# Moving the modulation chunks, the context entrance and two norms in a float32 model kernel

## The chip, the cores and the metric

One core of one Trainium2 chip runs the whole program. The metric is device microseconds of one execution; 2544.06 us is the median of three runs of the kernel before. The engines that matter here are PE (TensorE: matmuls, weight loads listed apart as PEld), ACT (ScalarE), DVE (VectorE) and SP, whose queue issues the loads.

## The reference, cut to what matters

256 tokens of 1024 channels pass through two parts. `first_block` is one layer: a norm, projections, a recurrence (`rwkv`) and a state-space branch (`s5`), gates, `w_out`, and a convolutional feed-forward:

```python
x = x + rms_norm(mixed, norm_mix_post[l])
h = rms_norm(x, norm_ffn_pre[l])
f = conv_ffn(h, ffn_w_up[l], ffn_conv_w[l], ffn_conv_b[l], ffn_w_down[l])
x = x + rms_norm(f, norm_ffn_post[l])
```

`second_block` has two layers with a second stream of 256 context tokens. Their inputs are modulated, `x * (1 + scale) + shift`, by `mod = silu_c @ w_ada[l] + b_ada[l]` (6144 values a layer, for the latent and for the context). Each layer has a linear attention (GLA), a latent attention (MLA), a 31-tap convolution, gates, an output projection and a feed-forward. All arithmetic is float32 in effect.

## The kernel before, in words

Activations are kept transposed: channels on the 128 partitions, tokens along the row (256, or 512 with the context as columns 256 to 511). Every dense product is three matmuls (`mm3`, L312 to L314), because both operands are split into a float32r high part and the rest: `w_high x_high + w_high x_low + w_low x_high`. A weight block of 512 KB is loaded into one of four `wraw` buffers, cast by ACT (`wh`, L276) and subtracted by DVE (`wl`, L277) into one of three pairs of buffers.

The modulation weights are 24 chunks of 512 columns (`ada`, L1035). A chunk is four `wraw` loads of 512 KB and eight matmuls of a 128x32 stationary tile with 512 columns (L1051), dealt to four column groups; the trace has 16 records for them. Up to LOTS = 4 chunks share one end: a copy of the row (L1057), four matmuls that fold it (8 records, L1061), small adds into `mod`. `ada` is a generator that yields after each half chunk. The chunks run in this order: 17 in lots of four beside the recurrence (`fill`, L442, called 62 times by `rwkv`; of three calls two advance `ada` and two the gate columns), one ahead of block 1's feed-forward (L508, `ADA[1]`), one between block 1 and layer 0 (L1806, `ADA[2]`), and one in each of the first five heads of layer 0's MLA (`beside`, L1218).

Block 1's end goes: `post` (L535) projects with `w_out`, scales and squares each tile on ACT, sums the squares over channels on PE (`colsum`, L363), then `rms_of` (L370) makes the reciprocal root in 11 small DVE operations and spreads it over 128 partitions by two transposes (L368). Eight times, two DVE operations then update X (L550, L551), and with `more` ACT squares X (L522) and PE sums again. `block1_ffn` makes its own root from these sums, `rms_in` (L525) normalises and splits X into `hh`, `hl` (L531, L304, L305), and `f_up` begins.

`enter` (L1782) modulates a stream and splits it into `hx`, the input of layer 0 (L1786, L304, L305). `enter(context, 1)` stands ahead of `block1_ffn` and loads the context through three buffers; `enter(X, 0)` stands behind it. Layer 0 begins with `conv_in` (L1354), whose first product is followed by `start` of `gla_gates` (L1446: `w_misc`); both are 512 columns wide.

The order on an engine isn't that of the text. The build puts it together from dependences and free buffers, earlier text first, so that an operation of later text stands ahead when the earlier one is not ready. `issue_after` adds an order edge.

Of the kernel before, what the change touches and what calls it, by code (L numbers as in the profile page):

```python
# [15 lines left out]
I32 = mybir.dt.int32  # L16
AF = mybir.ActivationFunctionType
# [4 lines left out]
P = 128  # L22
D = 1024
KT = 8
# [11 lines left out]
ADA = (17, 1, 1)  # L36
# [91 lines left out]
def const_arrays():  # L128
# [16 lines left out]
    c.raw("bcol", b2)  # L145

# [45 lines left out]
class Body:  # L192
# [23 lines left out]
    @contextmanager  # L216
    def behind(self, work):

        bb = self.nc.cur_bb
        n = len(bb.bb.instructions)  # L220
        work()
        mine = [i for i in bb.bb.instructions[n:] if i.engine == mybir.EngineType.DVE]
        if not mine:
            yield
            return
        with self.tc.issue_after(mine[-1]):
            yield

# [152 lines left out]
    def block1(self, X, xp):  # L381
# [4 lines left out]
        with ExitStack() as es:  # L386
# [52 lines left out]
            ada = self.ada(ADA[0], "sy", LOTS)  # L439
# [38 lines left out]
            return self.post(bp, X, "w_out", self.pairs(mh, ml), 0.5, "norm_mix_post", True)  # L478

    def block1_ffn(self, X, pc):  # L480
# [3 lines left out]
        with ExitStack() as es:  # L484
            bp = es.enter_context(tc.tile_pool(name="b1f", bufs=1))
            tp = es.enter_context(tc.tile_pool(name="b1ft", bufs=3))
            hh, hl = self.rms_in(bp, X, "norm_ffn_pre", self.rms_of(pc, 2, D, EPS))
# [20 lines left out]
            self.ada_all(ADA[1])  # L508
            self.dense("f_up", range(FT), self.pairs(hh, hl), epi_up)
            self.post(bp, X, "f_dn", self.pairs(gh, gl), 1.0, "norm_ffn_post", False)  # L510
# [9 lines left out]

    def squares(self, pc, X, sq, k):
        self.nc.scalar.activation(sq[:, k], X[:, k], AF.Square)  # L522
        self.colsum(pc, sq[:, k], k == 0, k == KT - 1)
# [11 lines left out]
    def post(self, bp, X, wname, x, scale, gname, more):  # L535

        nc = self.nc
        y, sq = self.b8(bp), self.b8(bp)
        pc = self.psum(2, "aux")

        def epi(m, ps):
            nc.scalar.activation(y[:, m], ps, AF.Copy, scale=scale)
            nc.scalar.activation(sq[:, m], ps, AF.Square, scale=scale)
# [4 lines left out]
        pc = self.psum(2, "aux") if more else None  # L548
        for k in range(KT):
            nc.vector.scalar_tensor_tensor(y[:, k], y[:, k], self.vc(1, gname, k), R, ALU.mult, ALU.mult)  # L550
            nc.vector.tensor_tensor(X[:, k], X[:, k], y[:, k], ALU.add)  # L551
            if more:
                self.squares(pc, X, sq, k)
        return pc
# [516 lines left out]
    def ada_all(self, n):  # L1071
        for _ in self.ada(n):
            pass

# [78 lines left out]
    def layer(self, l, g, mod, xd, xo, nxt, late):  # L1153
# [53 lines left out]
        with ExitStack() as es:  # L1207
            ya = self.gla(l, pool(es, "gla"), hx, hq, hb, V, full, *g.decay)
# [145 lines left out]
    def conv_in(self, l, pool, g, V, full, beside):  # L1354
# [79 lines left out]
    def gla_gates(self, l, pool, lp, hx, hb, V):  # L1434
# [11 lines left out]
        def start():  # L1446
            nc.sync.dma_start(wa, self.ap[f"w_wa{l}"])
            self.dense(f"w_misc{l}", [0], hx, lambda m, ps: nc.scalar.activation(misc, ps, AF.Identity, bias=V("b_misc", 0)))
# [42 lines left out]
    def gla(self, l, gp, hx, hq, hb, V, full, FB, Bt):  # L1491
# [35 lines left out]
        for h in range(4):  # L1527
# [4 lines left out]
            for m in (128, 64, 32, 16, 8, 4, 2, 1, 0):  # L1532
# [32 lines left out]
                else:  # L1565
# [3 lines left out]
                    else:  # L1569
                        nc.vector.copy_predicated(cd, mk[m][:, None, :].broadcast_to([P, 2 * n, 32]), ps)  # L1570
            for r in range(0, P, 32):
# [174 lines left out]
    def run(self):  # L1746
# [27 lines left out]
        with xs:  # L1774
            self.vload(1, "vec1", xp)
            pc = self.block1(X, xp)
# [3 lines left out]
            with tc.tile_pool(name="in0", bufs=1) as ip:  # L1780
# [13 lines left out]
                enter(context, 1)  # L1794
                self.vload("c2", "consts2", v2p)
                mk = self.t(v2p, ap["masks"].shape, tag="masks")
                nc.sync.dma_start(mk, ap["masks"])
                mk = mk.bitcast(I32)
                self.masks = {m: mk[:, i * 32 : i * 32 + 32] for i, m in enumerate((8, 4, 2, 1, 0))}
                self.vload("v20", "vec20", v2p)  # L1800
                self.vt["v21"] = self.t(v2p, ap["vec21"].shape, tag="v_v21")
                self.block1_ffn(X, pc)
# [3 lines left out]
                self.ada_all(ADA[2])  # L1806
# [137 lines left out]
```

## Time and profile before

| | |
|---|---|
| median of 3 runs (lowest to highest) | 2544.06 us (2539.36 to 2544.66) |
| the profiled execution, its own time | 2561.49 us |
| its span, first to last instruction | 2559.6 us |
| mean granted TensorE clock | 0.935 |
| busy, share of the span: PE, PEld, DVE, ACT | 97%, 83%, 71%, 49% |

Busy time of PE is modelled and pipelined: a matmul with 256 moving columns has a duration of 0.28 us, but in a dense stretch the next begins 0.12 us later. So the start of one matmul to the start of the next, and the chain of waits, tell what PE is held by; a busy share near 100% does not say that it runs at its peak.

### The profile page before, as it was taken

The page shows a single profiled execution, that of the slowest core. Times are in us where ns is not written, and L with a number is a line of the kernel's source. Part 1 is how long each engine was busy: PE and PEld are TensorE (multiplying, and loading weights), DVE is VectorE, ACT ScalarE, POOL GpSimd, SP SyncE. Part 2 cuts the span into 40 slices and gives each one's busy share as a digit, 9 for nine tenths or more (in the row PEclk, how much of TensorE's full clock was granted, in tenths as well). Part 3 has the DMA queues.
Part 4 walks back from the last instruction along what each step waited for, and adds up shares of the span by engine and source line. Part 5 has one row for each costly group of instructions (what it writes and reads, how often), then busy time and mean ns, then how long its engine had stood idle before and what let it go on. Part 6 is the DMA issues. An engine that isn't in the chain of part 4 may idle for free.

```text
span 2559.6 us, 45773 instructions
## 1 busy us (share of the span) xinstructions
PE 2478.7 (97%) x18348; PEld 2125.1 (83%) x18348; DVE 1815.5 (71%) x3376; ACT 1260.4 (49%) x2252; POOL 0.2 (0%) x4
## 2 busy tenths in 40 slices
PE   7999998999999999999999999999989999998998
PEld 7577888997788888666888898899978897798998
DVE  8575458855686778787646875656797788877884
ACT  5432246645455632455433654444556645555653
POOL 0000000000000000000000000000000000000000
PEclk9999898998999999999999899999989999998998
DMA  6666355654322122442335442256432332365663
GB/s 208 203 246 207 131 182 184 188 179 144 114 81 80 58 94 78 140 135 79 122 108 164 151 167 96 91 177 190 154 125 88 103 126 78 118 194 165 191 200 113
DMA packets 125780, 361.51 MB, mean 141 GB/s; under 512 B 14208, under 2 KB 39680, under 8 KB 125440
## 3 DMA queue, kind: packets, MB, share of 16 engines
q1 hardware_dynamic: 125568, 358.60, 43.6%
q8 instruction: 144, 2.36, 0.4%
q14 instruction: 68, 0.56, 0.1%
HBM read 344.08 MB, written 14.46 MB: 140 GB/s over the span
## 4 chain that ended last, share of the span: by engine, by line
PE 88%; DVE 6%; ACT 3%; DMA 2%; issue 1%; SPq 0%; ACTq 0%; DVEq 0%
PE mm L312 22%; PE mm L314 22%; PE mm L313 22%; PE aux L363 3%; PE aux L1720 2%; PE sy L1051 2%; PE sy L1733 1%; PE aux L1601 1%; PE aux L1719 1%; DVE wl L277 1%; PE aux L1557 1%; PE mm L1522 1%; PE mm L1520 1%; PE mm L1521 1%; PE aux L689 1%
## 5 line engine op out<-in xcount | busy, mean ns | idle before, releaser
L276 ACT CAST wh<-wraw 128x1024 fp32r<-128x1024 f32 (+3 forms) x544 | 543.4, 1000 | 756.4 <-PE mm L313 640.4
L277 DVE TENSOR_TENSOR wl<-wraw,wh 128x1024 fp32r<-128x1024 f32 (+3 forms) x544 | 631.2, 1161 | 332.1 <-ACT wh L276 319.9
L312 PE MATMUL mm<-hx,wh 128*128 128x256 f32 (+1 forms) x1792 | 607.2, 339 | 13.7 <-ACT hx L304 6.5
L314 PE MATMUL mm<-hx,wl 128*128 128x256 f32 (+1 forms) x1792 | 601.5, 337 | 4.7 <-DVE wl L277 4.5
L313 PE MATMUL mm<-hx,wh 128*128 128x256 f32 (+1 forms) x1792 | 603.7, 337 | 0.2 <-DVE hx L305 0.2
L312 PEld LDWEIGHTS mm<-hx,wh 128*128 128x128 f32 x1792 | 342.6, 191 | 56.0 <-ACT hx L304 7.3
L314 PEld LDWEIGHTS mm<-hx,wl 128*128 128x128 f32 x1792 | 341.4, 191 | 43.7 <-DVE wl L277 6.8
L313 PEld LDWEIGHTS mm<-hx,wh 128*128 128x128 f32 x1792 | 342.6, 191 | 39.0 <-issue 5.0
L1402 DVE SCALAR_TENSOR_TENSOR cv<-u,h_conv_dw,cv 128x512 f32<-128x512 f32 (+1 forms) x480 | 294.9, 614 | 8.6
L312 PE MATMUL mm<-b,wh 128*128 128x256 f32 x688 | 199.3, 292 | 4.7 <-ACT b L304 3.7
L314 PE MATMUL mm<-b,wl 128*128 128x256 f32 x688 | 197.0, 287 | 1.8 <-DVE wl L277 1.8
L313 PE MATMUL mm<-b,wh 128*128 128x256 f32 x688 | 196.2, 286 | 0.4 <-DVE b L305 0.3
L313 PE MATMUL mm<-gx,wh 128*128 128x256 f32 x528 | 148.1, 280 | 0.0
L314 PE MATMUL mm<-gx,wl 128*128 128x256 f32 x528 | 147.9, 280 | 0.0
L312 PE MATMUL mm<-gx,wh 128*128 128x256 f32 x528 | 147.7, 280 | 0.0
L312 PEld LDWEIGHTS mm<-b,wh 128*128 128x128 f32 x688 | 131.6, 192 | 17.6 <-issue 8.2
L313 PE MATMUL mm<-sp,wh 128*128 128x256 f32 (+1 forms) x448 | 141.1, 315 | 0.1
L314 PE MATMUL mm<-sp,wl 128*128 128x256 f32 (+1 forms) x448 | 140.8, 315 | 0.1
L312 PE MATMUL mm<-sp,wh 128*128 128x256 f32 (+1 forms) x448 | 140.7, 315 | 0.0
L314 PEld LDWEIGHTS mm<-b,wl 128*128 128x128 f32 x688 | 132.2, 192 | 7.2 <-DVE wl L277 3.3
L313 PEld LDWEIGHTS mm<-b,wh 128*128 128x128 f32 x688 | 132.4, 193 | 3.6 <-issue 2.1
L314 PEld LDWEIGHTS mm<-gx,wl 128*128 128x128 f32 x528 | 99.4, 188 | 0.0
(526 smaller groups left out, 4496.0 us busy)
## 6 DMA issues: line engine op xcount, KB each, us to landing
wraw<-w_up SPq DMA_DIRECT2D x100, 512.0 KB, 4.1
wraw<-w_ada SPq DMA_DIRECT2D x96, 512.0 KB, 4.6
wraw<-w_gates SPq DMA_DIRECT2D x48, 512.0 KB, 3.5
wraw<-w_dn SPq DMA_DIRECT2D x48, 512.0 KB, 3.8
wraw<-f_up SPq DMA_DIRECT2D x44, 512.0 KB, 3.6
wraw<-w_in SPq DMA_DIRECT2D x34, 512.0 KB, 4.0
wraw<-w_conv SPq DMA_DIRECT2D x32, 512.0 KB, 3.6
wraw<-w_o SPq DMA_DIRECT2D x24, 512.0 KB, 3.5
```

The lines of the kernel that those rows point to most:

```text
L276: nc.scalar.copy(h, raw)
L277: nc.vector.tensor_tensor(l, raw, h.bitcast(F32), ALU.subtract)
L312: mm(ps, wh, xh, start=first, stop=False)
L313: mm(ps, wh, xl, start=False, stop=False)
L314: mm(ps, wl, xh, start=False, stop=last)
L363: self.nc.tensor.matmul(pc[:, t : t + 1], sq[:, t * P : t * P + P], self.ones[:, 0:1], start=first and t == 0, stop=last and t == n - 1)
L689: mm(ps[q, i], lhs(8 * b + i, q), rhs(8 * b + i, q), start=True, stop=True)
L1051: nc.tensor.matmul(ps[q], self.sc[:, c : c + 32], w[:, i], start=j == 0 and k < nt, stop=j == len(lot) - 1 and k >= KT - nt)
L1402: nc.vector.scalar_tensor_tensor(r(o), u[:, :, j : j + S], dw(j), r(o), ALU.mult, ALU.add)
L1520: mm(ps, xh[:, tk], wh, start=kk == 0, stop=False)
L1521: mm(ps, xl[:, tk], wh, start=False, stop=False)
L1720: mm(ps, qr[hs, a], kr[hs, k0:], start=False, stop=True)
```

## The change

1. 19 chunks (not 17) run beside the recurrence, still in lots of four. The other five run in layer 0's GLA, in lots of four, half a chunk after the levels 128, 16 and 2 of each head. None is left ahead of the feed-forward, at layer 0's entrance or in MLA.
2. `post2` replaces `post` for `w_out`. It takes three sums over channels in the projection: of the squares of the mixed tile, of X times the scaled tile, and of the squares of the scaled tile. With the mean square of X kept from the first norm (`xx`) they give both roots, so that X is not squared and summed again.
3. `enter(context, 1)` and three constant loads move into `between`, whose ACT and DVE instructions are ordered behind the last ones of `f_up`.
4. In layer 0 the first product of `conv_in` and `w_misc` are made in two parts of 256 columns, the context's first.

```diff
-ADA = (17, 1, 1)
+ADA = 19
-    def dense_steps(self, name, chunks, x, epi, tok=None, cuts=()):
+    def dense_steps(self, name, chunks, x, epi, tok=None, cuts=(), parts=1):
...
-                ps = self.psum(ts.stop - ts.start)
-                for k, ((wh, wl), (xh, xl)) in enumerate(zip(w, x)):
-                    self.mm3(ps, wh, wl, xh[:, ts], xl[:, ts], k == 0, k == len(x) - 1)
-                    if k in cuts:
-                        yield
+                n = ts.stop - ts.start
+                ps = self.psum(n)
+                for p in reversed(range(parts)):
+                    q = slice(p * n // parts, (p + 1) * n // parts)
+                    for k, ((wh, wl), (xh, xl)) in enumerate(zip(w, x)):
+                        self.mm3(ps[:, q], wh, wl, xh[:, ts][:, q], xl[:, ts][:, q], k == 0, k == len(x) - 1)
+                        if k in cuts:
+                            yield
...
+                xx = self.t(bp, [P, 2], tag="xx")
+                nc.vector.tensor_scalar(xx, pc, 1.0 / D, EPS, ALU.mult, ALU.add)
...
-            return self.post(bp, X, "w_out", self.pairs(mh, ml), 0.5, "norm_mix_post", True)
+            return self.post2(bp, X, self.pairs(mh, ml), xx)
+
+    def post2(self, bp, X, x, xx):
...
+        cs = self.psum(S, "sy")
+        ones = self.ones[:, 0:1].broadcast_to([P, 32])
+        def epi(m, ps):
+            nc.scalar.activation(y[:, m], ps, AF.Copy, scale=gs[:, m : m + 1])
+            nc.scalar.activation(sq[0][:, m], ps, AF.Square, scale=0.5)
+            tt(sq[2][:, m], X[:, m], y[:, m], ALU.mult)
+            nc.scalar.activation(sq[1][:, m], y[:, m], AF.Square)
+            def sums():
+                for j in range(4):
+                    nc.tensor.matmul(cs[32 * j : 32 * j + 32], ones, sq[j % 3][:, m], start=m == 0, stop=m == KT - 1)
+            return sums
...
+        nc.scalar.copy(row, cs)
+        pc = self.psum(6, "aux")
+        for t in range(2):
+            nc.tensor.matmul(pc[:, 3 * t : 3 * t + 3], row[:, t * P : t * P + P], self.cc("pick"), start=True, stop=True)
+        pc = pc.rearrange("p (t s) -> p s t", s=3)
...
+        ts(v[0], pc[:, 0], 1.0 / D, EPS, ALU.mult, ALU.add)
+        r = self.rsqrt(v[0], 2)
+        R = self.psum(S, "aux")
+        for t in range(2):
+            self.rowcast(r, t, R[:, t * P : t * P + P])
+        w = v[1]
+        tt(w, r, pc[:, 1], ALU.mult)
+        stt(w, pc[:, 2], 2.0, w, ALU.mult, ALU.add)
+        tt(w, w, r, ALU.mult)
+        stt(w, w, 1.0 / D, xx, ALU.mult, ALU.add)
+        ts(w, w, EPS, None, ALU.max)
+        r = self.rsqrt(w, 2)
+        R2 = self.psum(S, "aux")
+        for t in range(2):
+            self.rowcast(r, t, R2[:, t * P : t * P + P])
+        for k in range(KT):
+            tt(y[:, k], y[:, k], R, ALU.mult)
+            tt(X[:, k], X[:, k], y[:, k], ALU.add)
+        return R2
...
-            self.ada_all(ADA[1])
             self.dense("f_up", range(FT), self.pairs(hh, hl), epi_up)
+            with self.after(mybir.EngineType.Activation), self.after(mybir.EngineType.DVE):
+                between()
...
+            ada = self.ada(len(self.adas), "sy", LOTS)
+            ya = self.gla(..., *g.decay, lambda m: m in (128, 16, 2) and next(ada, None))
+            deque(ada, 0)
...
         def beside(gp, i):
-            if l == 0:
-                self.ada_all(1)
             taps(gp)
...
-            for _ in self.dense_steps(f"w_conv{l}", [i], hq, epi):
+            for _ in self.dense_steps(f"w_conv{l}", [i], hq, epi, parts=n if i == 0 else 1):
...
-                enter(context, 1)
...
-                self.block1_ffn(X, pc)
+                self.block1_ffn(X, R, between)
...
                 enter(lambda k: X[:, k], 0)
-                self.ada_all(ADA[2])
```

(`w_misc` gets `parts=2 - l`; `gla` calls `fill(m)` at the end of each level.)

## Rows read from the trace of the kernel before

**Rows 1.** The page: busy time of the engines; shares of the chain that ended last.
```profile
PE 2478.7 (97%) x18348; PEld 2125.1 (83%) x18348; DVE 1815.5 (71%) x3376; ACT 1260.4 (49%) x2252; POOL 0.2 (0%) x4
...
PE 88%; DVE 6%; ACT 3%; DMA 2%; issue 1%; SPq 0%; ACTq 0%; DVEq 0%
```

**Rows 2.** Busy time in stretches; columns: stretch, length, engines (records), PEclk, DMA share, GB/s.
```profile
272.00:297.00 25.00, 25.00 (x287) 20.37 (x286) 7.72 (x27) 2.91 (x6) 0.00 (x0) 0.85 0.23 82
...
540.00:580.00 40.00, 40.00 (x344) 40.00 (x343) 16.57 (x15) 16.39 (x24) 0.00 (x0) 0.95 0.59 181
...
720.00:910.00 190.00, 189.26 (x1831) 160.70 (x1830) 137.10 (x208) 111.41 (x249) 0.00 (x0) 0.95 0.21 66
1040.00:1140.00 100.00, 98.14 (x451) 58.03 (x450) 76.47 (x140) 49.68 (x110) 0.00 (x0) 0.95 0.42 139
```

**Rows 3.** Chain of waits, w_out to f_up: start us, time on the chain, what.
```profile
371.84 0.12 PE mm L314
371.96 0.34 PE aux L363 x4
372.30 1.00 PE mm L1051 x2
...
374.89 3.46 DMA wraw<-f_up
378.43 1.04 ACT wh L276
...
379.85 6.85 PE aux L363 x32
386.76 2.65 DMA ix<-ctxT
...
390.15 2.87 DMA ix<-ctxT
```

**Rows 4.** Groups by form of DVE, 372 to 404 us.
```profile
L277 DVE TENSOR_TENSOR wl<-wraw,wh 128x1024 fp32r<-128x1024 f32 x3 | 3.6, 1219 | 0.0
...
L531 DVE SCALAR_TENSOR_TENSOR b<-X,v,aux 128x256 f32<-128x256 f32 x8 | 3.5, 472 | 0.5 <-PE aux L368 0.5
...
L551 DVE TENSOR_TENSOR X<-X,b 128x256 f32<-128x256 f32 x8 | 3.0, 417 | 0.0
```

**Rows 5.** Timeline of DVE at block 1's two ends: start us, us, instruction.
```profile
373.88 0.16 DVE L373 TENSOR_SCALAR rsv<-aux 128x2 f32<-128x2 f32 x1 [9.65 <-PE aux L363]
...
375.85 0.17 DVE L356 TENSOR_SCALAR rsy<-rsy 128x2 f32<-128x2 f32 x1
...
401.85 0.81 DVE L305 TENSOR_TENSOR b<-b,b 128x256 fp32r<-128x256 f32 x2
...
591.88 0.17 DVE L356 TENSOR_SCALAR rsy<-rsy 128x2 f32<-128x2 f32 x1
...
593.89 0.87 DVE L550 SCALAR_TENSOR_TENSOR b<-b,v,aux 128x256 f32<-128x256 f32 x2
...
605.47 0.41 DVE L305 TENSOR_TENSOR hx<-it,hx 128x256 fp32r<-128x256 f32 x1
```

**Rows 6.** Chain of waits, f_dn to layer 0: start us, time on the chain, what.
```profile
590.93 3.52 DMA wraw<-w_conv
...
598.92 0.95 ACT wh L276
...
606.15 0.23 PE mm L312
```

**Rows 7.** Busy time of L1051 alone in two stretches; columns: stretch, length, PE, PEld, PEclk, DMA.
```profile
70.00:270.00 200.00, 54.51 (x272) 7.94 (x272) 0.95 0.64 219
...
1040.00:1140.00 100.00, 12.12 (x80) 2.34 (x80) 0.95 0.42 139
```

**Rows 8.** The same of L1061 alone (the fold), second stretch.
```profile
1040.00:1140.00 100.00, 5.09 (x40) 5.04 (x40) 0.95 0.42 139
```

**Rows 9.** Line L1051's page: what PE sat idle for ahead of it (us, times).
```profile
  DMA wraw<-w_ada: 8.1, 11
```

More of the change, by code (lines that the diff above doesn't have):

```diff
@@ L145, in const_arrays @@
     c.raw("bcol", b2)
+    pick = np.zeros((P, 3), np.float32)
+    for s in range(3):
+        pick[32 * s, s] = 1
+    c.raw("pick", pick)
     j = np.arange(64)[:, None]
@@ L227, in behind, with after @@
             yield
+    def after(self, engine):
+        return self.tc.issue_after([i for i in self.nc.cur_bb.bb.instructions if i.engine == engine][-1])
     def dump(self, name, ap):
@@ L438, in block1 @@
             gates = self.dense_steps("w_in", range(9, 17), hx, epi_g, cuts=(2, 4))
-            ada = self.ada(ADA[0], "sy", LOTS)
+            ada = self.ada(ADA, "sy", LOTS)
             seq = [[gates, ada], [gates], [ada]]
@@ L477, in block1 @@
             branch(1, "w_bs", self.s5_glu(bp, tp, yg, half), 0.5)
-            return self.post(bp, X, "w_out", self.pairs(mh, ml), 0.5, "norm_mix_post", True)
-    def block1_ffn(self, X, pc):
+            return self.post2(bp, X, self.pairs(mh, ml), xx)
+    def post2(self, bp, X, x, xx):
+        nc = self.nc
+        tt, ts, stt = nc.vector.tensor_tensor, nc.vector.tensor_scalar, nc.vector.scalar_tensor_tensor
+        gs = self.t(bp, [P, KT], tag="gs")
+        ts(gs, self.v(1, "norm_mix_post")[:, :, 0], 0.5, None, ALU.mult)
+        y, sq = self.b8(bp), [self.b8(bp) for _ in range(3)]
+        cs = self.psum(S, "sy")
[9 more added lines that the diff above has]
+            return sums
+        self.dense("w_out", range(len(self.wtab["w_out"][1])), x, epi)
+        row = self.t(self.sm, [P, S], tag="arow", bufs=1)
+        nc.scalar.copy(row, cs)
[3 more added lines that the diff above has]
+        pc = pc.rearrange("p (t s) -> p s t", s=3)
+        v = [self.t(self.sm, [P, 2], tag="rsv2") for _ in range(2)]
+        ts(v[0], pc[:, 0], 1.0 / D, EPS, ALU.mult, ALU.add)
[17 more added lines that the diff above has]
+        return R2
@@ L481, in block1_ffn @@
+    def block1_ffn(self, X, R, between):
         self.nb8 = 5
@@ L533, in rms_in, with post @@
         return hh, hl
-    def post(self, bp, X, wname, x, scale, gname, more):
+    def post(self, bp, X, wname, x, gname):
         nc = self.nc
@@ L541, in epi @@
         def epi(m, ps):
-            nc.scalar.activation(y[:, m], ps, AF.Copy, scale=scale)
-            nc.scalar.activation(sq[:, m], ps, AF.Square, scale=scale)
+            nc.scalar.copy(y[:, m], ps)
+            nc.scalar.activation(sq[:, m], ps, AF.Square)
             return lambda: self.colsum(pc, sq[:, m], m == 0, m == KT - 1)
@@ L1069, in ada @@
                     nc.vector.tensor_scalar(mod[:, ms], mod[:, ms], 1.0 / ALPHA, None, ALU.mult)
-    def ada_all(self, n):
-        for _ in self.ada(n):
-            pass
     def modulated(self):
@@ L1207, in layer @@
         with ExitStack() as es:
-            ya = self.gla(l, pool(es, "gla"), hx, hq, hb, V, full, *g.decay)
+            ada = self.ada(len(self.adas), "sy", LOTS)
+            ya = self.gla(l, pool(es, "gla"), hx, hq, hb, V, full, *g.decay, lambda m: m in (128, 16, 2) and next(ada, None))
+            deque(ada, 0)
         rest = [i for i in range(KT) if i not in od]
@@ L1447, in start @@
             nc.sync.dma_start(wa, self.ap[f"w_wa{l}"])
-            self.dense(f"w_misc{l}", [0], hx, lambda m, ps: nc.scalar.activation(misc, ps, AF.Identity, bias=V("b_misc", 0)))
+            self.dense(f"w_misc{l}", [0], hx, lambda m, ps: nc.scalar.activation(misc, ps, AF.Identity, bias=V("b_misc", 0)),
+                       parts=2 - l)
         def gates(hs):
@@ L1489, in gla_gates, with gla @@
         return (FB, Bt), steps
-    def gla(self, l, gp, hx, hq, hb, V, full, FB, Bt):
+    def gla(self, l, gp, hx, hq, hb, V, full, FB, Bt, fill):
         nc = self.nc
@@ L1570, in gla @@
                         nc.vector.copy_predicated(cd, mk[m][:, None, :].broadcast_to([P, 2 * n, 32]), ps)
+                fill(m)
             for r in range(0, P, 32):
@@ L1792, in context, with between @@
                     return t
-                enter(context, 1)
-                self.vload("c2", "consts2", v2p)
                 mk = self.t(v2p, ap["masks"].shape, tag="masks")
[L1797 to L1801, printed above, removed]
-                self.block1_ffn(X, pc)
+                def between():
+                    enter(context, 1)
+                    self.vload("c2", "consts2", v2p)
+                    nc.sync.dma_start(mk, ap["masks"])
+                    self.vload("v20", "vec20", v2p)
+                    self.vt["v21"] = self.t(v2p, ap["vec21"].shape, tag="v_v21")
+                self.masks = {m: mk.bitcast(I32)[:, i * 32 : i * 32 + 32] for i, m in enumerate((8, 4, 2, 1, 0))}
+                self.block1_ffn(X, R, between)
                 self.dump("x2", X)
```

13 lines of the change are left out of this document (3 added, 10 removed).

## Prediction

> **What bounds the kernel now.** I read the page first: PE is busy for 97% of the span and holds 88% of the chain that ended last [rows 1]. Modelled busy time can't tell a stalled PE from a full one, so I took busy time by stretch next, and then the chain of waits where PE changes its work. In the feed-forward's projection (540 to 580 us) and in layer 0's linear attention (720 to 910 us) PE is busy throughout or but for 0.7 us, while DVE and ACT have room [rows 2]. The chain steps 0.12 us for a matmul of 256 columns and 0.23 us for one of 512 [rows 3, 6], so two halves cost what one whole does. Work taken off PE there is time saved, and work added is time lost. At block 1's two ends it is otherwise. There the chain leaves PE: behind `w_out` it waits 3.46 us for the load of `f_up`, then 2.65 and 2.87 us for context loads [rows 3]; behind `f_dn` it waits 3.52 us for `w_conv`, then for three casts, the last at 598.92 us [rows 6]. Both weight waits have one reason: the four buffers hold the four loads of the modulation chunk that stands there, and the next weights are issued only as its matmuls end.
>
> I sum against the profiled execution (2561.49 us, span 2559.6), which is 17.4 us above the median 2544.06; I take the savings as the same in both and subtract them from the median.
>
> **Norms and middle end.** Now the last matmul of `w_out` ends at 371.96 us [rows 3], the small chain begins at 373.88 [rows 5], and the last part of the normed X for `f_up` is there at 401.85 + 0.81 = 402.66 us [rows 5]. In the change the small chain begins later: one more ACT operation on the last tile, the sums, a row copy and two matmuls, less the 0.5 us that the chunk's first records stand in the way, so about 375.2 us. From there DVE is what is late. It has 26 small operations; eleven take 373.88 to 376.02, or 0.195 each [rows 5], so 5.1 us. Then 32 tile operations: scaling y and adding to X, 3.0 us for eight each, norm 3.5, split like the addition 3.0 [rows 4]: 12.5 us. That is 17.6 us and an end at 392.8; with 0.4 us for the hand-over of the second root, 393.2 us. The three `wl` subtractions (3.6 us) [rows 4], the eight context splits and the sums of X's squares (6.85 us on the chain) [rows 3] leave the gap. The weights can be cast before the projection ends, as nothing takes their buffers. 402.66 less 393.2 is 9.5 us; PE has less time to run ahead on the first tiles, so I take **8.5 us saved**, bounds 5 and 10.
>
> The projection itself pays a little. A tile's `colsum` is 0.34 us on the chain now [rows 3]. Four column groups of 256 columns replace it: between that 0.34 and the 1.0 us that a run of ada records with 512 columns takes even with only two of them [rows 3]. Half the columns is near the middle, 0.6. Seven tiles pay 0.25: **2 us lost**, bounds 0 and 5. The Trainium skill, TensorEngine Tiling (Array Packing), Key Properties, says that a change of tiling mode drains TensorE; by that the seven sums would lie nearer the upper bound and the term near 4 us. No row prices the drain by itself. The extra ACT operation (0.38 us) and the DVE one per tile lie beside some 3 us of matmuls. `xx` is one small operation in a long prologue: nothing.
>
> **Context entrance.** Behind `f_dn` the root is ready at 592.05, but X's first update begins at 593.89 [rows 5], because the fold of the chunk stands between. Without the chunk that is 1.7 us less, and its 0.5 us ahead of the sums goes too: X's updates begin about 592. Sixteen updates and eight splits follow, with no `wl` among them: about 9 us by the rows' means [rows 4], so the last part at 601.5 instead of 605.88 us [rows 5]: 4.4 us. Meanwhile PE can run ahead on the context's 24 matmuls (24 x 0.12 = 2.9 us), and on those of `w_misc` and the second tile if the build puts them forward: three tiles fill the three PSUM buffers, 8.6 us. PE does some of the first tile ahead of time now too, so the gain is between 0 and 8.6 us. With 4.4 that is 4.4 to 13; I take **9 us saved**, the middle, since the order does pull ready work forward (the cast of `f_up`'s block at 378.43 stands amid the norm's work) [rows 3]. If the cover is gone (weights not cast in time), the 3.5 us load wait is back. `enter(context)` now runs beside `f_dn`, where ACT and DVE are busy 16 of 40 us [rows 2]: 8 casts and 8 modulations hide there; the bound is the ACT work at once, 2 us. Its loads go past the weights on SP's queue; context buffers that come free late can hold the queue, and the three weight blocks already cast (24 x 0.12 us each) cover 8.6 us of that. The constants ride along at nothing for the same reason; their first readers come in layer 0.
>
> **Chunks.** In MLA five chunks cost 12.12 us of L1051 and 5.09 us of folds [rows 7, 8]: 17.2 us. In the linear attention five chunks in two lots need ten halves, 1.0 us each when not broken up [rows 3], 2.0 when the order breaks it in two, and two folds of 1.0: 12.0, at worst 22. The likeliest is near the unbroken price, 12.7: **4.5 us saved**, bounds -5 and 6. Beside the recurrence two more chunks cost 54.51 / 17 = 3.2 us each [rows 7] at most, 1.1 us per half unbroken at least; its last part, 272 to 297 us, keeps PE busy throughout [rows 2], so little hides: **4.5 us lost**, bounds 2 and 6.5.
>
> **Sum.** -8.5 + 2 - 9 - 4.5 + 4.5 = -15.5 us: 2544.06 - 15.5 = 2528.5 (2546 for a profiled execution like the one shown).
>
> **Rivals.** (a) *Less put forward.* The first product alone runs ahead, and halves are broken up in the attention: savings of 5 + 4.4 + 3, losses of 3 + 5.5: 4 us in all, 2540. For it: DVE is a hard floor at both ends; against: the order already mixes stages. Half-way to it is 2534.
>
> (b) *Everything put forward*: 10 + 13 + 6 - 1 - 2 = 26, 2518.
>
> (c) *MLA had room.* Weight loads keep PE busy only 58 of 100 us in MLA but 160.7 of 190 in the linear attention [rows 2]. If that is the slack, five chunks were partly hidden where they were and are dear where they go: no saving in MLA, 12.7 us of cost, against 4.5 us of saving assumed: 2528.5 + 17.2 = 2546, no change. Against it: the chain of MLA is long float32 matmuls with few weights, and PE is busy 98 of 100 us. The Trainium skill, Perfetto Trace Analysis, Identifying the Most-Contended Engine, says just this: judge TensorE's headroom by LDWEIGHTS share, not by matmul busy time. By that rule the chunks move from room to none.
>
> (d) *Slower: loads in the attention.* Each half brings two 512 KB loads into the four buffers just ahead of weights. At block 1's ends such a load set back the next weights by 3.46 and 3.52 us [rows 3, 6]. If each of ten halves did so in the attention, 35 us: 2528.5 + 35 = 2563.5. It decides from 1.6 us a half up. Against it: L1051 waited for loads only 8.1 us in 11 places [rows 9], and three cast blocks of 24 matmuls (5.6 us each) stand ahead.
>
> **How the numbers follow.** My forecast, by itself 2520 to 2536, has 0.62; (a) 0.16, half-way included; (b) 0.07; (c) 0.08; (d) 0.07. Faster means below 2539, slower above 2549 (0.2% is about what a measurement of this kernel can tell from no change). All of the forecast and (b) and 0.13 of (a) are faster: 0.82. The rest of (a) and (c) are the same: 0.11. (d) is slower: 0.07. The range from 2515 to 2543 leaves out the far end of (b), most of (c), and (d).
>
> **What would show it.** Right: no chunk and no wait for `f_up` or `w_conv` in the chain at the two ends; the last parts of the normed and of the modulated X some 9.5 and 4.4 us sooner after their projections than now; matmuls of 256 columns of `w_conv` right behind `f_dn`; MLA shorter by about 17 us and the attention longer by about 13. Wrong: waits for `w_ada` or weights ahead of the attention's matmuls; MLA as long as before; the projection's tiles longer by 0.6 us or more; idle PE at the start of `f_dn`.

## The result, and the profile after

The changed kernel takes 2571.09 us (median of 4 runs, 2560.87 to 2578.10) beside 2544.36 for the kernel before on the same chip: ratio 1.0103, 95% interval 1.0060 to 1.0145. It is slower by 26.7 us, where 15.5 us less was forecast. The range, 2515 to 2543, does not hold it.

The first trace of the kernel before had a span of 2559.6 us at a granted clock of 0.935, 15 us above the median of its runs, so it was profiled once more, without a change. That trace has a span of 2536.6 us at 0.981; the changed kernel's has 2573.6 at 0.973. Stages are compared with this fresh trace.

> The kernel before, unchanged, for a second trace of it on the same chip: its first profiled execution stood 17 us above the median of its runs, at a granted clock of 0.935, so stage differences against it were understated. Expected: the same stages, and where the clock is granted in full a span nearer 2545 us; GLA of layer 0 (first query/key epilogue to last gate epilogue, 717.68 to 906.51 in the first trace) at 189 us within 3.

The linear attention took 187.0 us in it, within the 3 us expected; the time was 2538.5. From the starts of the instructions that end each stage:

| stage | before, fresh trace | after | difference |
|---|---|---|---|
| start to the last addition of the mixed branches (`mix`) | 342.2 | 357.1 | +14.9 |
| to the first result of `f_up` (middle end) | 56.8 | 49.9 | -6.9 |
| `f_up` | 115.1 | 119.5 | +4.4 |
| to the first query/key of layer 0's GLA (entrance) | 191.9 | 183.8 | -8.1 |
| GLA of layer 0, to the last gate result | 187.0 | 222.6 | +35.6 |
| to the last product of MLA | 310.4 | 306.3 | -4.1 |
| the rest | 1333.3 | 1334.5 | +1.2 |
| span | 2536.6 | 2573.6 | +37.0 |

(`f_up` is not touched. It took 119.5 us in the first trace of before too, and 115.1 in the traces of runs 1 and 3 below, with the changed norms: that term is not the change's. These are single traces; for the first stage, experiment 5 has more of them.)

The page after, in the lines of [rows 1], and PE's line in the fresh trace of before:

```profile
PE 2477.0 (96%) x18384; PEld 2120.8 (82%) x18384; DVE 1817.8 (71%) x3390; ACT 1258.1 (49%) x2248; POOL 0.2 (0%) x4
...
PE 86%; DVE 7%; ACT 4%; issue 1%; DMA 1%; SPq 0%; ACTq 0%; DVEq 0%
```
```profile
PE 2456.0 (97%) x18348; PEld 2111.8 (83%) x18348; DVE 1815.1 (72%) x3376; ACT 1261.0 (50%) x2252; POOL 0.2 (0%) x4
```

PE is busy 21.0 us longer than in the fresh trace, in a span 37.0 us longer, and the chain runs a little more through DVE and ACT; these lines do not say where. The stretches do (columns as in [rows 2]): GLA and the stretch inside MLA after, then GLA in the fresh trace of before.

```profile
710.18:932.77 222.59, 207.48 (x1928) 166.67 (x1926) 137.65 (x208) 112.51 (x256) 0.00 (x0) 0.95 0.31 105
1040.00:1140.00 100.00, 97.51 (x412) 66.11 (x411) 85.36 (x144) 47.88 (x106) 0.00 (x0) 0.98 0.20 59
```
```profile
705.97:892.92 186.95, 186.02 (x1835) 158.85 (x1833) 135.97 (x199) 111.15 (x253) 0.00 (x0) 1.00 0.22 69
```

Before, PE lacked 0.9 us of the 187.0 in GLA; now it lacks 15.1 of 222.6, and its busy time is 21.5 us longer, partly at the lower granted clock (0.95 in the mean). The waits of PE in GLA after (us in all, times, longest):

```profile
PE aux L1611 <- DVE eqk L1598: 7.1, 9, 1.7
PE mm L320 <- ACT wh L284: 2.7, 4, 0.8
...
PE sy L1108 <- DMA wraw<-w_ada: 0.7, 2, 0.4
```

The chunks' own loads are waited for 0.7 us only. The longest wait is that of the levels (L1611) for DVE's `eqk`, which the change does not touch. The timeline of PE in head 0 shows why it comes to light:

```profile
722.85 1.16 PE L1611 MATMUL aux<-eqk 128*128 128x128 f32 x8
723.93 1.06 PE L1108 MATMUL sy<-wraw,sc 128*32 128x512 f32 x8
725.08 0.69 PE L1611 MATMUL aux<-eqk 128*64 128x64 f32 x16
726.12 1.05 PE L1108 MATMUL sy<-wraw,sc 128*32 128x512 f32 x4 [0.35 <-DMA wraw<-w_ada]
727.35 0.46 PE L1611 MATMUL aux<-eqk 128*32 128x32 f32 x32 [0.18 <-DVE eqk L1598]
727.64 1.04 PE L1108 MATMUL sy<-wraw,sc 128*32 128x512 f32 x4
729.63 0.46 PE L1611 MATMUL aux<-eqk 128*32 128x32 f32 x32 [0.94 <-DVE eqk L1598]
730.85 0.50 PE L320 MATMUL mm<-hx,wh 128*128 128x512 f32 x1 [0.77 <-ACT wh L284]
```

A level is one operation on DVE (1.22 us), its exponentials on ACT (1.34 us) and one more on DVE (1.22 us), so that even with two levels overlapped one comes every 2.3 to 2.7 us. Before, that time was filled: between the levels of head 0 stand 60 matmuls of the next head's projection, 13, 7, 8, 9 and 9 in a row of 512 columns each, then 14, most of 256. After, 13 are left, and half a chunk takes the place of some. The displaced projection follows later, with no level to hide. And in the three stretches of levels, heads 0 to 2, the clock of 2.4 GHz fell to its other level, 1.2, for a part of the time (columns as above; the clock is the third number from the right), where the fresh trace of before has 1.00 over all of GLA:

```profile
720.00:745.00 25.00, 21.09 (x290) 13.47 (x290) 18.77 (x22) 16.55 (x42) 0.00 (x0) 0.86 0.55 196
778.00:805.00 27.00, 22.30 (x287) 14.15 (x286) 20.97 (x24) 17.18 (x43) 0.00 (x0) 0.81 0.50 176
838.00:862.00 24.00, 19.03 (x290) 12.79 (x289) 19.58 (x31) 16.56 (x40) 0.00 (x0) 0.86 0.41 146
```

SP's timeline says why the projection is not there: the weights' loads, after and then before (fresh trace).

```profile
688.05 0.33 SPq L273 DMA_DIRECT2D wraw<-w_ada  x1
694.89 6.06 SPq L273 DMA_DIRECT2D wraw<-w_ada  x2
706.05 0.33 SPq L273 DMA_DIRECT2D wraw<-w_ada  x1
722.94 0.80 SPq L273 DMA_DIRECT2D wraw<-w_ada  x2
725.03 0.80 SPq L273 DMA_DIRECT2D wraw<-w_qk  x2
727.21 1.83 SPq L273 DMA_DIRECT2D wraw<-w_v  x2
```
```profile
683.84 0.33 SPq L265 DMA_DIRECT2D wraw<-w_qk  x1
...
701.84 0.33 SPq L265 DMA_DIRECT2D wraw<-w_v  x1
```

The four raw buffers that come free while head 0's own projection runs went to the next head's `w_qk` and `w_v`. Now they go to one chunk, whose first matmuls come at 721.85 us, behind the first level. So the chunk sits in the buffers for up to 34 us, and the first weights are issued 14.9 us after GLA's first query/key instead of 22.1 us ahead of it: 37 us later.

### The profile page after: what moved, and what is told of

Its sections match the earlier page's. It is cut to its first block, busy times and chain, and to the rows that moved or that the text cites. A ratio compares the mean times of both kernels' runs of the same rounds, so it can differ in the third digit from the quotient of the medians.

```text
span 2573.6 us, 45867 instructions
## 1 busy us (share of the span) xinstructions
PE 2477.0 (96%) x18384; PEld 2120.8 (82%) x18384; DVE 1817.8 (71%) x3390; ACT 1258.1 (49%) x2248; POOL 0.2 (0%) x4
## 4 chain that ended last, share of the span: by engine, by line
PE 86%; DVE 7%; ACT 4%; issue 1%; DMA 1%; SPq 0%; ACTq 0%; DVEq 0%
PE mm L320 22%; PE mm L322 22%; PE mm L321 21%; PE aux L374 2%; PE sy L1108 2%; PE aux L1775 2%; PE sy L1788 2%; DVE wl L285 2%; PE aux L1656 1%; PE aux L1774 1%; DVE cv L1455 1%; PE mm L1576 1%; PE mm L1575 1%; PE mm L1574 1%; PE aux L746 1%
## 5 line engine op out<-in xcount | busy, mean ns | idle before, releaser
L320 PEld LDWEIGHTS mm<-hx,wh 128*128 128x128 f32 x1816 | 347.3, 192 | 54.0 <-ACT wh L284 8.2
L322 PEld LDWEIGHTS mm<-hx,wl 128*128 128x128 f32 x1816 | 347.2, 192 | 42.0 <-DVE wl L285 6.8
L321 PEld LDWEIGHTS mm<-hx,wh 128*128 128x128 f32 x1816 | 347.6, 192 | 36.4 <-issue 3.8
```

The costliest lines, as they stand in the source:

```text
L320: mm(ps, wh, xh, start=first, stop=False)
L321: mm(ps, wh, xl, start=False, stop=False)
L322: mm(ps, wl, xh, start=False, stop=last)
```

## Experiments

Theory A: the chunks' loads take the raw buffers that the next head's weights need, and its projection no longer fills the waits between the levels. Theory B: the chunks' own matmuls are the price.

**1. The chunks out of GLA.** The rest of the change stays.

```diff
-            ada = self.ada(len(self.adas), "sy", LOTS)
-            ya = self.gla(l, pool(es, "gla"), hx, hq, hb, V, full, *g.decay, lambda m: m in (128, 16, 2) and next(ada, None))
-            deque(ada, 0)
+            ya = self.gla(l, pool(es, "gla"), hx, hq, hb, V, full, *g.decay, lambda m: None)
...
         def beside(gp, i):
+            if l == 0:
+                deque(self.ada(1), 0)
             taps(gp)
```

> The changed kernel with its last five modulation chunks taken out of the linear attention of layer 0 and put into the latent attention there, one per head; the 19 beside the recurrence, the norms and the entrance stay. Theory A (the chunks' weight loads hold the four raw weight buffers, so the next head's projection comes into TensorE's order too late to stand between the levels of this head): the linear attention goes from 222.6 us back to 189 to 191, the latent attention takes some 8 to 17 us more, the time is 16 to 26 us below the changed kernel's, 2545 to 2555. Theory B (the chunks' own matmuls, and the drains around them, are the price, wherever they stand): the time stays within 5 us of the changed kernel's. Theory C (the loss is in the recurrence, the two more chunks there): within 8 us of the changed kernel's, since the recurrence is the same.

2541.0 us (10 runs), ratio to before 0.9983 (0.9965 to 1.0002): 30 us below the changed kernel. GLA is back to 186.6 us:

```profile
703.87:890.49 186.62, 185.68 (x1835) 158.70 (x1833) 135.97 (x199) 111.15 (x253) 0.00 (x0) 1.00 0.22 69
```

B and C fall. A has the direction and the place; its numbers were too small (16 to 26 us for the time), and MLA took only 4.6 us more than in the change (310.9 after 306.3) where A had 8 to 17. What is left of the change is no clear gain over the kernel before.

**2. Products without loads, then loads with a quarter of the products.** The first diff is the run without loads, the second the other.

```diff
-                for w in self.wraws(f"w_ada{l}", ch):
+                for w in self.resident() if self.still and l == 1 else self.wraws(f"w_ada{l}", ch):
```
```diff
-                        nc.tensor.matmul(ps[q], self.sc[:, c : c + 32], w[:, i], start=j == 0 and k < nt,
+                        e = P if self.still else 512
+                        nc.tensor.matmul(ps[q, :e], self.sc[:, c : c + 32], w[:, i, :e], start=j == 0 and k < nt,
```

> The changed kernel, where the five chunks in the linear attention multiply a tile that is already in SBUF in place of their weights: their loads are left out (and with them the right modulation values), their matmuls, folds and places are kept. Theory A: dense matmuls of the next head stand between the levels again, the linear attention takes 189 plus the matmuls' own 5 to 13 us, 194 to 202 us, and the time falls by 20 to 28 us against the changed kernel. Theory B (the matmuls themselves): the linear attention stays at 217 to 223 us and the time within 5 us of the changed kernel's.

> The changed kernel, where the five chunks in the linear attention load all their weights but multiply 128 of every 512 columns (three quarters of those products are left out). It is the counterpart of the run without loads. Theory A: the order on TensorE stays as thin of dense work between the levels as in the changed kernel, the linear attention stays at 213 to 223 us, and the time falls by 0 to 8 us, what the columns themselves take. Theory B: it goes most of the way back, to 195 us or below, and the time falls by over 20 us.

Without loads 2545.26 us, ratio 0.9996 (0.9979 to 1.0014); with the loads and a quarter of the columns 2575.13, ratio 1.0104 (1.0072 to 1.0136), as slow as the whole change. GLA in the first, then in the second with its groups of PE (busy, mean ns | idle ahead of them):

```profile
709.56:907.04 197.48, 195.94 (x1910) 161.91 (x1908) 137.86 (x208) 112.86 (x255) 0.00 (x0) 1.00 0.21 65
```
```profile
710.08:936.42 226.34, 204.37 (x1931) 169.83 (x1929) 137.58 (x208) 111.92 (x256) 0.00 (x0) 0.90 0.30 103
...
L1614 PE MATMUL aux<-eqk 128*32 128x32 f32 (+2 forms) x768 | 23.5, 234 | 9.2 <-DVE eqk L1601 9.1
...
L1109 PE MATMUL sy<-wraw,sc 128*32 128x128 f32 x80 | 5.5, 305 | 2.6 <-DMA wraw<-w_ada 2.6
```

Theory A holds in both, though the second is not faster at all and its GLA is 3.3 us above A's bound. The products cost 197.5 - 187.0 = 10.5 us in GLA; ten of the 80 records run as early as 600 us there, so all of them would cost about 12 (an estimate, 10.5 x 80 / 70), near the forecast's 12.7. The other 25 us hang on the loads: in the change PE is idle 13.6 us longer than without loads (15.1 and 1.5) and busy 11.5 us longer (207.48 and 195.94), at a granted clock of 0.95 in place of 1.00. With the chunk's records 8 us shorter, the levels and the weights are only waited for longer.

**3. The same loads at the end of each head.**

```diff
-            ya = self.gla(..., lambda m: m in (128, 16, 2) and next(ada, None))
+            ya = self.gla(..., lambda: [next(ada, None) for _ in range(3)])
...
             if h < 3:
                 cur = project(h + 1)
+            fill()
```

> The changed kernel with the same five chunks in the linear attention of layer 0, same loads and matmuls, but asked for after the next head's projection (three halves at the end of each head) in place of between the levels. It tells the place of the loads in the queue from their number. Theory A (a load of a chunk that stands ahead of the next head's weights makes these late): head 0 gets its dense work between the levels back, heads 1 to 3 only in part, because the halves issued at the end of a head still stand ahead of the weights of the one after; the linear attention takes 200 to 212 us against 222.6, and the time falls by 10 to 22 us against the changed kernel. Theory A' (it is the number of loads on four buffers, wherever they stand): within 6 us of the changed kernel.

2562.62 us, ratio 1.0063 (1.0046 to 1.0081): 8.5 us below the changed kernel (10 by the two ratios), at the edge of A's 10 and outside the 6 of A'. GLA took 217.6 us, more than A's 212. Head 0 got its filling back (its stretch to the next head's query/key 26.9 us after 49.5), but heads 1 and 2 took 71.0 and 57.0 us, where the fresh trace of before has 48.8 and 48.7.

**4. A buffer of their own.** 2.1 KB a partition are left in GLA, half of a raw block, so the chunk is loaded by k-tile.

```diff
+                raw = self.t(self.own_pool, [P, 1, c], tag="araw", bufs=1)
+                self.nc.gpsimd.dma_start(raw, src[:, i : i + 1])
```

> The changed kernel, where the chunks in the linear attention of layer 0 load into a raw buffer of their own (one k-tile of 2 KB a partition, in the 2.1 KB that are left there), issued from GpSimd's queue; same bytes, same matmuls, same places asked for. It tells the four shared raw buffers from the bytes. Theory A1 (a chunk's load takes a raw buffer and a place in the queue ahead of the next head's weights): the linear attention goes from 222.6 us to 195 to 205, as in the run without loads (197.5), and the time falls by 18 to 28 us against the changed kernel's. Theory A2 (the bytes: chunk and weights share what the DMA engines move, and the weights are late whatever buffer the chunk has): the linear attention stays above 212 us and the time within 10 us of the changed kernel's.

> The same with those loads on SyncE's queue, where the weights' loads are issued too: a chunk's load that waits for its one buffer now holds back the weights' loads behind it in the queue. Theory A1a (the buffers alone): as the run with a buffer of its own on GpSimd's queue within 4 us. Theory A1b (the place in the queue): the linear attention takes 205 us or more and the time is 6 us or more above that run's.

Both were slower than the change: 2597.74 (ratio 1.0199, 1.0174 to 1.0225) and 2586.40 (1.0155, 1.0131 to 1.0179), with 252.3 and 235.8 us in GLA. One reason is that a product now comes alone; PE's timeline:

```profile
720.05 1.05 PE L1117 MATMUL sy<-araw,sc 128*32 128x512 f32 x2
721.03 1.16 PE L1622 MATMUL aux<-eqk 128*128 128x128 f32 x8
```

Two records on one column tile hold PE from 720.05 to 721.03, 0.98 us; in the change eight on four column tiles took 1.0 (721.85 to 722.85). So the chunk was laid out anew, 128 columns of four k-tiles in one buffer:

```diff
+                raw = self.t(self.own_pool, [P, 4, P], tag="araw", bufs=1)
+                for i, (off, kk, c) in enumerate(blocks[b : b + 2]):
+                    self.nc.gpsimd.dma_start(raw[:, 2 * i : 2 * i + 2], src[:, :, e : e + P])
```

> The run with a buffer of its own on GpSimd's queue mended: that one gave each matmul of a chunk a load and a place of its own, so that a lone product of 512 columns took 0.98 us where four on four column tiles take 1.0 us together, 37.4 us for 40 of them against 15.3. Here one buffer holds 128 columns of four k-tiles, and the four matmuls of a load stand together again. Same bytes, same products. Theory A1 (buffers and queue): the linear attention goes from 222.6 us to 195 to 208, the time falls by 14 to 28 us against the changed kernel's 2571. Theory A2 (bytes): above 214 us, and within 8 us of the changed kernel's.

> The same with the loads on SyncE's queue, ahead of the next head's weights where a load waits for its one buffer. Theory A1a (the four shared buffers alone): within 4 us of the run on GpSimd's queue. Theory A1b (the place in the queue): 6 us or more above it.

2601.51 (1.0224, 1.0173 to 1.0275) and 2583.87 (1.0168, 1.0124 to 1.0212), with 254.1 and 239.9 us in GLA: no version met its number, so the time settles nothing here. The traces do. PE's waits in GLA of the first; two more of 0.6 and 0.2 us, for `rsy` and `att`, are all the others. Below them, SP's first load for the next head:

```profile
PE sy L1104 <- DMA araw<-w_ada: 21.2, 28, 2.9
```
```profile
690.09 0.33 SPq L273 DMA_DIRECT2D wraw<-w_qk  x1
```

With the same bytes and a buffer of their own, neither the levels nor the weights are waited for. The first weights are issued 22.1 us ahead of GLA's first query/key (712.22 us), as in the fresh trace of before, and 22.1 us ahead in the last run too, with the loads on SP's queue. And the dense work is back between the levels (matmuls of the next head's projection there, counted in the timelines of PE):

| | head 0 | head 1 | head 2 |
|---|---|---|---|
| before, fresh trace | 60 | 73 | 73 |
| the change | 13 | 13 | 4 |
| the change without the chunk's loads | 60 | 49 | 64 |
| a quarter of the chunk's columns, all loads | 13 | 13 | 15 |
| a buffer of its own, four runs | 43 to 48 | 58 | 58 |

So neither the bytes (A2) nor the queue sets the weights back; the shared buffers do, as A1 has it. With the loads on SP's queue the time is 11 and 18 us below that on GpSimd's, against A1b. No run shows A1 by its time, because the layout has a price of its own: one buffer brings 2.9 to 21.2 us of waits for itself, and the chunk in pieces costs more than whole. PE's timeline:

```profile
770.79 0.28 PE L1597 MATMUL mm<-wl,hx 128*128 128x256 f32 x1
770.99 0.41 PE L1104 MATMUL sy<-araw,sc 128*32 128x128 f32 x4
771.33 0.38 PE L1595 MATMUL mm<-wh,hx 128*128 128x256 f32 x1
771.56 0.28 PE L1596 MATMUL mm<-wh,hx 128*128 128x256 f32 x1
```

Two of a load's four products (four records) hold PE for 0.34 us, and the dense matmul on either side of them for 0.20 and 0.23 in place of 0.11. Four whole raw buffers for the chunk would need 16 KB a partition; that wasn't tried, for want of room.

**5. The two chunks in the recurrence.**

```diff
-ADA = 19
+ADA = 17
```

The second run has `ADA = 12`; the rest stands in layer 0's MLA, one a head in the first, two a head in the second.

> The changed kernel with 17 chunks beside the recurrence, as in the kernel before, and the other seven in the latent attention of layer 0, one per head; norms and entrance as in the change. It measures the two chunks in the recurrence against the run with 19 there and five in the latent attention (2541.0 us). Theory A (TensorE is busy throughout in the recurrence, each chunk there costs its 3.1 to 3.9 us; in the latent attention five chunks of 17 us gave back only 4 to 9 us when they left, so one costs 1 to 2 us): 3 to 6 us faster than with 19, 2535 to 2538 us, 8 to 11 us below the kernel before. Theory B (two chunks cost the recurrence the 11 to 15 us by which it ended later in the traces, clock and all): 8 to 12 us faster, 2529 to 2533. Theory C (a chunk costs the same 3.4 us anywhere): within 2 us of 2541.

> The same with 12 chunks beside the recurrence (those that layer 0 reads) and 12 in the latent attention of layer 0, two per head in one lot with one fold for both. Theory A (3.1 us a chunk in the recurrence, 1 to 2 us in the latent attention): 5 to 10 us faster than with 17 and 7. Theory C (the latent attention's room is used up by the first five, and each more costs its full 3 us): within 3 us of the run with 17 and 7, or slower.

2543.77 (ratio 0.9990, 0.9976 to 1.0004) and 2548.07 (1.0009, 0.9996 to 1.0022) beside 2541.0 with 19 and 5: A and B fall in the first, C is missed by 0.8 us; in the second A falls and C holds. In the traces the recurrence's last output product (L808) comes at 304.6, 296.4 and 285.8 us with 19, 17 and 12 chunks, so there the last two cost 4.1 us each and the five ahead of them 2.1. Where the stage of the table ends, at `mix`'s last addition, it is more: 357.0, 346.5 and 337.9 us, so 5.3 and 1.7 each. Over all traces but the first of before, `mix` ends at 342.2 to 348.3 us with 17 chunks (six traces) and at 354.5 to 358.7 with 19 (ten), 11.6 us apart in the mean. From GLA's end to layer 0's `w_up` it is 534.5, 545.9 and 564.9 us with 5, 7 and 12, so there they cost 5.7 and 3.8 each. What one place gives the other takes. The chunk's line in the recurrence, 70 to 300 us, with 19 (the change) and 17 (fresh trace of before, then the run with 17 and 7; columns as in [rows 7]):

```profile
70.00:300.00 230.00, 62.97 (x304) 8.95 (x304) 0.98 0.65 220
```
```profile
70.00:300.00 230.00, 54.15 (x272) 7.87 (x272) 0.99 0.60 204
```
```profile
70.00:300.00 230.00, 56.19 (x272) 8.04 (x272) 0.98 0.59 202
```

32 records more take 6.8 to 8.8 us, 3.4 to 4.4 a chunk. That leaves 3 to 5 of the 11.6 us that are not the chunks' own matmuls; the granted clock from 300 to 345 us is 0.92 with 19 chunks and 0.96 and 1.00 in these two traces with 17, but how much of the rest that is, no run tells.

**6. The parts alone.** Norms alone and entrance alone are the change's hunks on the kernel before; chunks alone is

```diff
-ADA = (17, 1, 1)
+ADA = (19, 0, 0)
```

and the fourth run is the change with all seven chunks back where before has them.

> The kernel before with one part of the change alone: block 1's two middle norms from one set of sums; the chunks stay 17, 1, 1 and 5, the entrance as before. The prediction gave this part, with the chunk that left that place, 6.5 us net (8.5 at the middle end, less 2 in the projection). Theory A (the gain in the changed kernel's trace at this place, 7 to 8 us, is the norms'): 4 to 8 us faster than the kernel before. Theory B (it is the chunk's, which stood in the same place): within 3 us of the kernel before.

> The kernel before with its two chunks at block 1's ends put beside the recurrence (19 there, five in the latent attention as before); norms and entrance as before. With the run of the norms alone (2546.0 us, no gain) it tells whether the two share one gain at the middle end. Theory A (two chunks more cost the recurrence 8 us, and at the ends of block 1 they stood in time that nothing else used): 0 to 5 us slower than the kernel before. Theory B (they cost 3.4 us where they stood, as anywhere): within 3 us of it. In the trace, the stretch from the mix's last addition to f_up's first result is to fall by under 2 us if the norms' chain sets it, by 5 if the chunk does.

> The kernel before with the entrance alone: context columns between block 1's two dense parts, the first projections of layer 0 in two halves, context first; chunks and norms as before. The prediction gave the whole entrance 9 us, with the chunk that left it. Theory A (the gain of 8 to 10 us in the changed kernel's trace is the entrance's): 4 to 9 us faster than the kernel before. Theory B (it is the chunk's that stood there): within 3 us of it.

> The changed kernel with all seven moved chunks put back where the kernel before has them (17, one before f_up, one at the entrance, five in the latent attention); norms and entrance as in the change. If the chunk at each end only fills a wait that the norms and the entrance shorten, it now stands on the path: theory A, 0 to 5 us faster than the kernel before, no better than the run with 19 and 5 in the latent attention (2541.0). Theory B (the parts add up as the prediction had them: 8.5 and 9 us, less the two chunks): 10 us faster or more.

The ratio is to runs of the kernel before made beside each (2545.15 us for the norms, 2546.04 for run 1, 2547.86 for the others).

| on the kernel before | us | ratio (95%) | middle end | entrance |
|---|---|---|---|---|
| nothing (fresh trace) | | | 56.8 | 191.9 |
| norms alone | 2546.04 | 0.9999 (0.9986 to 1.0011) | 54.7 | 192.5 |
| two chunks to the recurrence alone | 2557.89 | 1.0039 (1.0023 to 1.0055) | 54.2 | 191.9 |
| entrance alone | 2550.25 | 1.0012 (0.9995 to 1.0029) | 55.2 | 195.7 |
| norms and entrance, chunks as before | 2545.59 | 0.9990 (0.9977 to 1.0003) | 51.3 | 195.6 |
| all three, five chunks in MLA (run 1) | 2541.00 | 0.9983 (0.9965 to 1.0002) | 50.0 | 181.8 |

Norms alone and entrance alone gain nothing (B in both). The chunks alone lose 10 us, more than either theory had, although the middle end is 2.6 us shorter (between the 2 and the 5 that were to tell norms from chunk): so they cost the recurrence some 12 us, as in experiment 5. The fourth run is 2.3 us faster than before, theory A. With the two chunks gone, norms and entrance together are worth 0.0056 of the time, 14 us with some 6 of uncertainty (run 1 beside the chunks alone); the two stages of these traces have 14.3. At the entrance it is plain: the chunk away alone gives 0, the new order alone loses 3.8, both give 8 to 10. PE's waits there, 560 to 640 us, with the entrance alone and in the change, each with SP's loads behind it:

```profile
PE mm L316 <- ACT wh L280: 4.9, 3, 2.5
PE mm L318 <- DVE wl L281: 1.2, 1, 1.2
```
```profile
567.17 8.55 SPq L269 DMA_DIRECT2D wraw<-w_ada  x4
584.69 0.33 SPq L269 DMA_DIRECT2D wraw<-w_conv  x1
```
```profile
PE mm L321 <- DVE hx L313: 1.3, 1, 1.3
```
```profile
575.92 0.33 SPq L273 DMA_DIRECT2D wraw<-w_conv  x1
```

With the chunk the first load of `w_conv` is issued 2.9 us ahead of X's first update (587.62 us), without it 19.8 us ahead (595.74). While the chunk stands there, its loads hold the buffers, the weights are cast late, and work that is ready sooner has no weights. The two chunks then cost the recurrence most of what their going made possible.

**7. The chunks in PE's waits.** 17 beside the recurrence, three in MLA, two at layer 0's last norm, two at layer 1's norm behind the mix.

```diff
             self.ln(lf, x, S, EPS / 2, sums[st], beside)
+            if l == 0 and st == full[-1]:
+                deque(self.ada(2, "mm", 2), 0)
```

> The changed kernel's norms and entrance with 17 chunks beside the recurrence and the other seven put where TensorE waits: three in the latent attention of layer 0, two at the end of layer 0's feed-forward while its last norm runs (TensorE was idle 5.0 of the 10 us from 1840 in the fresh trace of the kernel before), two at layer 1's norm after the mix (idle 6.9 of the 20 us from 2310). Theory A (a chunk is 3.4 us of TensorE's time wherever TensorE is the bound, and nearly nothing where it waits): 8 to 14 us faster than the run with 17 and 7 (2543.8), 2530 to 2536 us, faster than both kernels. Theory B (the chunk's loads push the next weights back there as in the linear attention, and the stall only moves): within 4 us of 2543.8, or slower.

2545.99 us, ratio 0.9995 (0.9979 to 1.0011): theory B. MLA and what follows it to `w_up` became 20.7 us shorter than with seven chunks there, and from the end of `w_up` in layer 0 to its start in layer 1 it became 24.7 us longer. PE's waits from 1640 to 1960 us (the run with 17 and 7 has 2.5 us for `wh` there and none for `w_ada`):

```profile
PE mm L320 <- ACT wh L284: 5.0, 2, 4.9
PE mm L1108 <- DMA wraw<-w_ada: 4.5, 3, 2.4
```

A place where PE waits is not free when the next weights must come through the same buffers. No version beat the kernel before by more than its measurement is uncertain; the nearest is run 1.

## Why the prediction was wrong

**Chunks from MLA to GLA: -4.5 forecast, +30 measured** (the change beside run 1). This step failed, and makes 34.6 of the 42.6 us between forecast and result. Its GLA half priced the chunk by PE's time for it, 12.7 us; that price was right (10.5 to 12 without loads). What it left out was named in rival (d), at 0.07: each half brings two loads ahead of the weights. It was set aside because three cast blocks stand ahead of the waits. But the loads do not delay by the 3.5 us that one takes: they hold all four buffers until their matmuls are due, 34 us, and the weights' lateness is paid as levels without cover and a lower granted clock, with hardly a wait for a load to be seen. Rival (d)'s 35 us came near in size by luck: it counted ten waits for loads, and what the loads took away was the cover. The prediction took a PE that is busy throughout for one that only its own matmuls hold; it did not ask what the dense work itself was hiding.

The MLA half was too large: 17.2 us of chunk and fold went, and the stretch from GLA's end to MLA's last product became 4.1 us shorter. PE's waits there grew from 1.8 to 5.8 us, with `pr` and `vm` of ACT at their head (3.5 and 1.4 us), and the clock was granted at 0.98 in the stretch shown above, 1.00 in the fresh trace of before. Without loads in GLA, at 1.00, it became 9.0 us shorter. Rival (c) had this side right: between a quarter and a half of the 17.2 us came back. The Trainium skill, Perfetto Trace Analysis, Identifying the Most-Contended Engine, judges room by the LDWEIGHTS share. That share (58 of 100 us in MLA, 160.7 of 190 in GLA [rows 2]) did point to MLA, and the trace agrees.

**Two chunks in the recurrence: +4.5 forecast, bounds 2 and 6.5; 8.2 us** in the recurrence's last output product and **11.6** at `mix`'s end, between the traces with 19 and 17. This term was mis-sized, and makes 7 of the other 8 us: 3.2 us a chunk [rows 7] was taken as a ceiling, but it is a mean of PE's time for 17 chunks alone; the last two take 3.4 to 4.4 each in their own matmuls, and the stage grows by more than these.

**Norms and middle end: -8.5 and +2 forecast, -6.9 in the trace.** Right in both terms: from `mix`'s end to the sums of the last tile it is 28.7 us in place of 26.4, so the projection lost 2.3 (nearer the 2 taken than the 4 weighed against it), and from there to `f_up`'s first result 21.1 in place of 30.4. The chain of waits after shows the steps: the norm's DVE work starts behind the second root and ends with the last part split near 398.5 us, and no load of `f_up` stands in the chain.

```profile
390.77 0.68 PE aux L379 x2
...
397.92 0.49 DVE b L592
398.48 0.41 ACT b L312
398.94 1.01 PE mm L320 x3
```

But the gain was the chunk's going as much as the norms', which alone were worth 2.1 there and nothing in the time.

**Entrance: -9 forecast, -8.1 in the trace**, and the wait for `w_conv` is gone from the chain. Right, with the same condition: only together with the chunk.

So by trace the two ends give 15.0 us, near the 15.5 of the forecast, and the recurrence takes 11.6 of them: 3.4 us are left where the forecast had 11, and by time run 1 has 4 to 5 us, not certain. With the 30.1 of the move to GLA, -15.0 + 11.6 + 30.1 = 26.7 us, the measured difference, closer than single traces can be trusted to.

## What to carry to other kernels

Before putting loads of other work ahead of a stretch, count how long they will hold the shared buffers until their use, not how long a load takes, and ask which later weights those buffers were feeding. Where a dense stretch shows no idle time, look at what its matmuls hide: take them away and a chain on the other engines comes to light. Parts that shorten waits at one place are to be costed together; what stands in a wait is free only until the wait goes.

## What was not expected of the hardware

A product on one of four column tiles cost as much alone (0.98 us for two records) as four on four tiles together (1.0 us). The Trainium skill, TensorEngine Tiling (Array Packing), Key Properties, says that tiles work independently and in parallel, and that a change of mode drains TensorE. Both fit these rows and the 0.20 and 0.23 us of the dense matmuls beside such products, though no run here separates the drain from the rest.

The same loads into one buffer, issued from GpSimd's queue, were waited for 21.2 us, and from SP's 12.2 us (13.7 and 2.9 with lone products).
